# A decoder layer whose issue order is computed: other assumed costs for matmuls, small products and scans

## The chip, the cores and the metric

The kernel runs on one core of one Trainium2 chip. The time is device microseconds (us) of one execution. A core has a tensor engine (PE, with the loading of weights shown apart as PEld), a vector engine (DVE), a scalar engine (ACT), GpSimd (POOL) and SyncE (SP), which here starts the transfers (DMA). Each engine works through its own list of instructions in order; between engines, an instruction waits until what it reads has been written and what it overwrites has been read.

## The reference

One layer on 512 tokens of width 1024: a half-step gated feed-forward part (FFN 1), a mixer, cross-attention into 256 memory tokens, and a second half-step feed-forward part (FFN 2), each with a norm before and after. The mixer is where the change acts. It has eight heads of forgetting attention and four of a gated delta rule:

```python
def causal_conv_silu(x, w):                    # four taps over the tokens, then silu
    ...
cq, ck, cv = jnp.split(qkv, ...)               # after the convolution
q = l2_norm(cq...);  k = l2_norm(ck...)
beta = jax.nn.sigmoid(gb)
g = -jnp.exp(gdn_a_log) * jax.nn.softplus(ga + gdn_dt_bias)
...
L = jnp.where(strict, jnp.einsum('bhncd,bhnsd->bhncs', k_beta, k) * decay, 0.0)
A = L + jnp.eye(CHUNK)
u = lax.linalg.triangular_solve(A, v_beta, left_side=True, lower=True)
w = lax.linalg.triangular_solve(A, k_beta * jnp.exp(g)[..., None], left_side=True, lower=True)
...                                            # then a scan over the chunks of tokens
```

## The kernel before, in words

Large products are made in float32 by three float32r passes: a weight block of 128 x 1024 (`raw`) is split into a high part (`wh`, by ACT) and a low part (`wl`, by DVE, or now and then by POOL, see `nblock`), activations likewise, and PE multiplies high by high, low by high and high by low. Products run over 512 columns in the feed-forward parts, over 256 or 512 in the mixer.

The mixer, in the program's order:

- Gates (lines 771 to 870). A small product gives the logits; they are put in `zr`, turned by four PE transposes, worked on by DVE, ACT and POOL in `gw` (128 x 64), put in `yd`, turned back, and summed along the tokens by scans (`gc`, 128 columns a piece; `Fc`, 512 columns).
- Keys of four heads. The convolution adds three taps by DVE and one by POOL in `cy`; ACT takes a tanh into `cth`; DVE forms `co`. The same three tiles serve queries and values (`qv`, line 1005). `cR`, `cV`, `qe` and other small columns come from `smalls`, of which some are a power that POOL takes (`mhalf` is the exponent -1/2).
- The inverse of `A` (from line 990). The 32-row diagonal blocks of all heads go through memory, a block to a partition (`Lb`), and are solved by 31 steps on DVE: `Wb` is a product, `Tb` the update. The result returns by a DMA to `T` and is transposed by DVE to `X`. Products of 32 and of 64 rows on PE then double the blocks. `vb` are the values times beta, by ACT.
- The scans over chunks, the heads of forgetting attention, the output product, the mixer's last norm (`h`, `xn`), whose rows PE transposes (`xt`). The keys of the memory (`km`, from `mT`) are computed beside the last norm.

No engine's order is written out. Every instruction goes through the class `Issue`, which keeps what it reads and writes (`add`, line 119) and gives it an assumed cost in ns by its engine, its kind and its size (lines 159 to 177). `place` (line 190) puts instructions on the engines by these costs, of those ready the most urgent first; `settle` (line 226) does this ten times, backwards and forwards by turns, takes the result with the shortest assumed span, and ties each engine's instructions to that order. `AFTER` holds the assumed time from an instruction's end to the start of one that waits for it; `TICK` and `COLUMNS` model the PE clock. Some instructions are issued through `TK`, `VK`, `AK` and `QK`, which keep the order in which they are written. Because all instructions are called from one helper, every row of the profile has line 270 before, and 273 after; tiles tell them apart.

Of the kernel before, what the change touches and what calls it, by code (L numbers as in the profile page):

```python
# [17 lines left out]
S = 512  # L18
# [20 lines left out]
class Issue:  # L39
    """The order in which the engines issue.  # L40

    Every instruction is kept with what it reads and writes. At the end they are placed on the
    engines by a rough cost, backwards and forwards by turns, of those ready the most urgent
    first, and each engine gets its instructions in that order (as dependencies that need no
    semaphore).
    """

    # from the end of an instruction to the start of one that waits for it: on the same engine,
    # on the tensor engine, on another
# [7 lines left out]
    # the tensor engine's clock is halved after a tick with too few columns  # L57
    TICK, COLUMNS = 3413.3, 3072

    def __init__(self, tc):  # L60
        self.tc = tc
        self.ins = []
        self.unit = []  # the engine or queue that is held
        self.kind = []  # what the next one waits for
        self.cost = []
        self.columns = []
        self.pred = []
        self.writer = {}
        self.readers = {}
        self.bank = {}  # L70
        self.rings = {}
        self.first = {}
        self.touched = {}
        self.before = {}
        self.ring_of = {}
        self.grain = {}
        self.kept, self.after = {}, {}

    def engine(self, engine, unit, ordered=False):
        """ordered: what is issued through it keeps its order"""  # L80
        return _Issuer(engine, unit, self, ordered)

    def tile(self, pool, shape, dt, tag, bufs=1, name=None, grain=(32, 32)):
        """a tile, told apart by pieces of so many rows and columns"""
# [10 lines left out]
    def cells(self, x):  # L95
        """name, pieces touched, rows, free size"""
# [22 lines left out]
    def add(self, ins, unit, op, fp32):  # L119
# [4 lines left out]
        for group, cells_of, size_of in ((ins.ins, reads, sizes[0]), (ins.outs, writes, sizes[1])):  # L124
            for x in group:
# [5 lines left out]
                if name.startswith("psum"):  # L131
                    # one after another on a bank
# [31 lines left out]
        elif unit == "PE":  # L164
            passes = 4 if fp32 and op == "matmul" else 2 if fp32 else 1
            cost = max(size * passes * 0.41667, cols * 0.8333) + 2.6
# [3 lines left out]
        elif unit == "DVE":  # L170
            single = op != "transpose" and len(sizes[0]) - scalars == 1 and not psum
            cost = 68 + size * (6.3 if op == "reciprocal" else 0.521 if single else 1.042) + 61 * scalars
# [11 lines left out]
    def keep(self, unit):  # L184
        """the last instruction stays behind the last kept one of its engine"""
# [4 lines left out]
    def place(self, edges, waits, urgency, clock=False):  # L190
        """start of each instruction, on each unit the most urgent ready one first"""
# [68 lines left out]
class _Issuer:  # L260
    """an engine whose instructions are kept"""
# [19 lines left out]
def tile_decoder_layer(  # L281
# [38 lines left out]
    # slots of [128, 512], handed out by hand  # L320
# [20 lines left out]
    def move(src, dst, n=None):  # L341
        """free slots from one ring to another"""
# [14 lines left out]
    def bank(*ids):  # L357
        """the next PSUM bank of a ring of banks"""
# [20 lines left out]
    # that of some instructions stays as written  # L379
# [33 lines left out]
    def rstd_of(s0, s1):  # L413
        """(s0 + s1 + eps) ^ -1/2"""
# [16 lines left out]
    def wblock(ap):  # L431
        """now and then Pool takes the low part"""
# [10 lines left out]
    # the first loads, in the order in which they are needed  # L443
# [28 lines left out]
    def prenorm(src, g, dst):  # L472
        """rms_norm of a block of 128 rows, transposed and split into dst(half, part)."""
# [17 lines left out]
    def proj_t(wb, xT, ps, sl, first=True, by=1, mm=mm):  # L491
        """transposed product: ps[:, sl] += w_block^T x^T (float32 by three float32r passes, each
        over so many k at a time)."""
# [20 lines left out]
    def nat_product(ks, lhs, wdram, nh, evac, ntail, ts=tuple(range(NT)), last=None):  # L514
        """natural product: out[t, n*512:] = sum_k lhs(k)[:, t]^T w[k]; evac(n, t, ps).
        The last ntail blocks of k (two k each) finish the row blocks one after another."""
# [35 lines left out]
    def residual_epilogue(gidx, weight, nxt, final=False):  # L552
        """evac callback: h += weight * rms_norm(product) * gain; then nxt(t)."""
# [82 lines left out]
    # ================= FFN 1 =================  # L636
    xT = new_xT()

    def lead_in(ps, xT):
        """the first products, of rows not normed yet; returns the rows' factors, in all partitions"""  # L640
# [78 lines left out]
    # ================= mixer =================  # L719
# [30 lines left out]
    # wmt order: gates, gk of all heads, (gq, gv) per head, (fq, fk) per pair  # L750
# [20 lines left out]
    # gates: each of four groups of 32 rows holds a decay logit, two forget logits and a beta  # L771
    # logit, four rows each, and the same again for the low part of the weights; the logarithms are worked out by token, [128 tok, chunk, group, kind]
# [57 lines left out]
    def aug(src):  # L830
        """rows (-hi, -lo, 1, 1) and (1, 1, hi, lo) of a logarithm, whose product is its difference"""
# [15 lines left out]
    # per-token columns [128 tok, chunk, head]  # L847
# [49 lines left out]
    # the 32-row diagonal blocks of each head go through DRAM, a block to a partition and back  # L897
    NB = 32 * S + 32  # from a diagonal block to the next one of its 128 tokens
# [22 lines left out]
    def decay(pg, hh, which, dst):  # L921
        """exp of the decay between two tokens of a chunk: [query, key], or its transpose"""
# [23 lines left out]
    # keys of all heads: convolved, silu-ed, transposed [channel, token]; L of each head  # L946
# [43 lines left out]
    # T = (I + L)^-1, X = T^T: the diagonal blocks of all heads by substitution, with a block  # L990
    # to a partition; then blocks are doubled twice by products
# [13 lines left out]
    def qv(hh):  # L1005
        """queries and values; attention inside a chunk (transposed)"""
# [31 lines left out]
    def inverse(hh):  # L1038
# [17 lines left out]
        # blocks of 32 rows doubled, those of rows 0-63 and of rows 64-127  # L1056
# [515 lines left out]
```

## Time and profile before

| | before |
|---|---|
| timed runs | 1224.33, 1222.79, 1224.20 us, median 1224.2 us |
| profiled execution, span of the instructions | 1222.4 us |
| PE busy | 1192.9 us (98%) |
| PE loading weights | 1002.6 us (82%) |
| DVE busy | 642.7 us (53%) |
| ACT busy | 493.0 us (40%) |
| POOL busy | 128.6 us (11%) |
| DMA | 120.32 MB, 98 GB/s |
| chain that ended last | PE 87%, DVE 7%, DMA 2%, issue 2%, ACT 2% |
| mean granted PE clock | 0.995 of full speed |

The shares are averages over the whole span, in which stages with different limits lie. The profiled execution is one of many; its span runs from the first to the last instruction, and the timed runs hold what lies around it too.

In a timeline, a row is the start in us, the time of one group in us, the engine, the line, the operation, the tile written and the tiles read with their shapes, and how many instructions the row holds; in brackets the idle time before it and what ended that. A matmul's time holds its pass through the array, and the next begins before it ends; its cost in a stream of matmuls is the interval between starts.

### The profile page before, as it was taken

What the parts mean: (1) busy time and instruction counts of PE and PEld (TensorE: products, weight loads), DVE (VectorE), ACT (ScalarE), POOL (GpSimd) and SP (SyncE); (2) the same over time, 40 slices, a digit from 0 to 9 for tenths busy, and PEclk for the clock granted to TensorE, in tenths of its full rate; (3) what the DMA queues carried; (4) which work ended last, traced back from release to release, by engine and by line L of the source; (5) the groups of instructions that cost most, each with busy time, mean ns of one, the idle gap of its engine ahead of it and who ended that gap; (6) DMA issues with size and microseconds to landing.
All of it is one profiled execution on the core that took longest, in us unless ns stands there. A gap on an engine that the chain in (4) does not pass through costs nothing.

```text
span 1222.4 us, 15630 instructions
## 1 busy us (share of the span) xinstructions
PE 1192.9 (98%) x6078; PEld 1002.6 (82%) x6078; DVE 642.7 (53%) x1152; ACT 493.0 (40%) x1024; POOL 128.6 (11%) x121
## 2 busy tenths in 40 slices
PE   7999999999999899899999999999999999999997
PEld 7888888888888687788787888888988888888886
DVE  5655455442327979469975744546634334342323
ACT  5323223222226564368974644435422323222221
POOL 1000000000001432222020442012000000000000
PEclk9999999999999999999999999999999999999999
DMA  5332322333333231211214253222432332333321
GB/s 192 122 100 90 103 88 102 103 103 104 109 101 104 87 113 57 91 54 54 73 60 164 91 181 118 79 67 65 125 103 88 102 97 93 104 107 100 102 71 69
DMA packets 41753, 120.32 MB, mean 98 GB/s; under 512 B 9424, under 2 KB 9680, under 8 KB 41680
## 3 DMA queue, kind: packets, MB, share of 16 engines
q1 hardware_dynamic: 41168, 119.20, 30.9%
q8 instruction: 47, 0.77, 0.3%
q0 software_dynamic: 512, 0.13, 0.1%
q14 instruction: 26, 0.21, 0.1%
HBM read 114.73 MB, written 4.46 MB: 98 GB/s over the span
## 4 chain that ended last, share of the span: by engine, by line
PE 87%; DVE 7%; DMA 2%; issue 2%; ACT 2%; SPq 0%; POOL 0%; DVEq 0%; POOLq 0%; ACTq 0%
PE psum L270 87%; DVE Wb L270 1%; DVE Tb L270 1%; DMA mr<-in_mem_dram 1%; DVE wl L270 1%; DVE gw L270 1%; DMA raw<-in_wkvk_dram 1%; DVE co L270 1%; DVE xn L270 1%; DVE cy L270 0%; SPq L270 0%; DMA h<-in_x_dram 0%; DVE smalls L270 0%; DVE pt L270 0%; DVE h L270 0%
## 5 line engine op out<-in xcount | busy, mean ns | idle before, releaser
L270 PE MATMUL psum<-xt,wh 128*128 128x512 f32 (+1 forms) x2064 | 599.4, 374 | 0.3 <-ACT wh L270 0.2
L270 PEld LDWEIGHTS psum<-xt,wh 128*128 128x128 f32 x2064 | 373.6, 190 | 63.5 <-ACT wh L270 0.5
L270 ACT ACTIVATE wh<-raw 128x1024 fp32r<-128x1024 f32 (+1 forms) x202 | 213.0, 1056 | 526.0 <-PE psum L270 293.3
L270 PE MATMUL psum<-xt,wl 128*128 128x512 f32 (+1 forms) x1016 | 376.6, 375 | 0.8 <-DVE wl L270 0.7
L270 DVE TENSOR_TENSOR wl<-raw,wh 128x1024 fp32r<-128x1024 f32 (+1 forms) x176 | 216.3, 1230 | 275.8 <-ACT wh L270 275.2
L270 PEld LDWEIGHTS psum<-xt,wl 128*128 128x128 f32 x1016 | 190.9, 190 | 32.7 <-DVE wl L270 1.2
L270 PE MATMUL psum<-wh,hh 128*128 128x512 f32 x352 | 137.1, 390 | 0.0
L270 PE MATMUL psum<-wl,hh 128*128 128x512 f32 x352 | 137.1, 390 | 0.0
L270 PE MATMUL psum<-wh,hl 128*128 128x512 f32 x352 | 137.0, 389 | 0.0
L270 POOL TENSOR_TENSOR smalls<-smalls,mhalf 128x1 f32<-128x1 f32 (+1 forms) x38 | 26.5, 700 | 789.8 <-ACT smalls L270 784.0
L270 PEld LDWEIGHTS psum<-wh,hh 128*128 128x128 f32 x352 | 66.1, 188 | 13.8
L270 PEld LDWEIGHTS psum<-wh,hl 128*128 128x128 f32 x352 | 66.1, 188 | 13.6
L270 PEld LDWEIGHTS psum<-wl,hh 128*128 128x128 f32 x352 | 66.1, 188 | 13.6
L270 POOL TENSOR_TENSOR wl<-raw,wh 128x1024 fp32r<-128x1024 f32 x26 | 63.7, 2450 | 120.8 <-ACT wh L270 110.2
L270 PE MATMUL psum<-wh,xt 128*128 128x512 f32 x128 | 43.5, 409 | 0.4 <-DVE q L270 0.4
L270 DVE SCALAR_TENSOR_TENSOR hv<-s,psum 128x512 f32<-128x512 f32 x22 | 15.1, 688 | 53.7 <-PE psum L270 53.5
L270 DVE TENSOR_TENSOR tu<-psum,rb 128x512 f32<-128x512 f32 x22 | 15.2, 692 | 53.4 <-PE psum L270 53.3
L270 DVE TENSOR_TENSOR fg<-psum,gbc 128x512 f32<-128x512 f32 x32 | 22.0, 688 | 37.1 <-ACT u L270 37.1
L270 DVE TENSOR_TENSOR tg<-psum,rb 128x512 f32<-128x512 f32 x22 | 15.2, 692 | 44.5 <-PE psum L270 44.5
L270 ACT ACTIVATE u<-psum 128x512 f32<-128x512 f32 x32 | 19.0, 593 | 41.4 <-PE psum L270 41.4
L270 ACT ACTIVATE hh<-hv 128x512 fp32r<-128x512 f32 x44 | 27.4, 623 | 16.2 <-DVE hv L270 16.2
L270 DVE TENSOR_TENSOR hl<-hv,hh 128x512 fp32r<-128x512 f32 x44 | 30.1, 685 | 1.5 <-ACT hh L270 1.5
(232 smaller groups left out, 1431.3 us busy)
## 6 DMA issues: line engine op xcount, KB each, us to landing
raw<-in_f2gu_dram SPq DMA_DIRECT2D x44, 512.0 KB
raw<-in_f1gu_dram SPq DMA_DIRECT2D x43, 512.0 KB
raw<-in_f1d_dram SPq DMA_DIRECT2D x22, 512.0 KB
raw<-in_f2d_dram SPq DMA_DIRECT2D x22, 512.0 KB
raw<-in_wmt_dram SPq DMA_DIRECT2D x21, 512.0 KB
gbc<-in_gains_dram SPq DMA_DIRECT2D x16, 256.0 KB
raw<-in_wmn_dram SPq DMA_DIRECT2D x8, 512.0 KB
raw<-in_wout_dram SPq DMA_DIRECT2D x8, 512.0 KB
```

What stands on the lines that cost most here:

```text
L270: r = call(*args, **kw)
```

## The change

Three of the assumed costs are different; nothing else of what the program does is. For a float32r matmul (one pass) PE's constant is 13.3 ns in place of 2.6. A float32 matmul (four passes) with inputs of at most 32 rows counts half. A scan of DVE counts 2.04 ns per element in place of 1.042. The diff's other lines remove comments and docstrings.

```diff
         elif unit == "PE":
             passes = 4 if fp32 and op == "matmul" else 2 if fp32 else 1
-            cost = max(size * passes * 0.41667, cols * 0.8333) + 2.6
+            cost = max(size * passes * 0.41667, cols * 0.8333) + (13.3 if passes == 1 else 2.6)
+            if passes == 4 and rows <= 32:
+                cost /= 2
             columns = size * passes * rows / 128
...
         elif unit == "DVE":
             single = op != "transpose" and len(sizes[0]) - scalars == 1 and not psum
-            cost = 68 + size * (6.3 if op == "reciprocal" else 0.521 if single else 1.042) + 61 * scalars
+            each = {"reciprocal": 6.3, "tensor_tensor_scan": 2.04}.get(op, 0.521 if single else 1.042)
+            cost = 68 + size * each + 61 * scalars
```

The program has the same instructions before and after. Their order on PE, DVE, ACT, POOL and SP differs from about 350 to 880 us of the span; the feed-forward parts are practically as they were. Two places follow.

DVE at the gates, before: the end of the gate chain. `gw_430` are the gates, `yd_431` their copy for the transposes back, `co_460` a head's keys after the convolution, `cy_466` the taps of the next head, `smalls_63` small columns.

```order
L270 SCALAR_TENSOR_TENSOR gw_430_2964<-gw_430_2964 128x64 x7
L270 TENSOR_TENSOR gw_430_2964<-gw_430_2964 128x64
L270 TENSOR_TENSOR gw_430_2964<-gw_430_2964,coef_2750 128x64
L270 SCALAR_TENSOR_TENSOR co_460_3110<-cth_459_3104,cy_458_3102 128x512
L270 COPY yd_431_2988<-gw_430_2964 128x16x16
L270 TENSOR_SCALAR smalls_63<-smalls_63 128x4
L270 SCALAR_TENSOR_TENSOR cy_466_3154<-psum_64,cw_2744,cy_466_3154 128x511
```

The same place now:

```order
L273 SCALAR_TENSOR_TENSOR gw_430_2964<-gw_430_2964 128x64 x3
L273 SCALAR_TENSOR_TENSOR cy_466_3154<-psum_64,cw_2744,cy_466_3154 128x511
L273 SCALAR_TENSOR_TENSOR gw_430_2964<-gw_430_2964 128x64
L273 SCALAR_TENSOR_TENSOR cy_466_3154<-psum_64,cw_2744,cy_466_3154 128x510
L273 TENSOR_TENSOR gw_430_2964<-gw_430_2964 128x64
L273 TENSOR_TENSOR smalls_63<-smalls_63 128x4
L273 TENSOR_TENSOR cV_455_3078<-smalls_63,bN_2967 128x4
L273 TENSOR_TENSOR gw_430_2964<-gw_430_2964,coef_2750 128x64
L273 TENSOR_TENSOR smalls_63<-smalls_63,bN_2967 128x4
L273 COPY yd_431_2988<-gw_430_2964 128x16x16
```

The two `cy_466` steps and four small ones on `smalls` and `cV` stood behind `yd` and now stand ahead of it; `co_460` is further up. On PE, 17 more matmuls of 256 columns stand ahead of the transposes of `zr`, and between these and those of `yd` there are 37 matmuls of 256 columns and 29 of 512 in place of 54 and 17.

DVE at the first steps of the substitution, before. `Wb_449` and `Tb_3047` are its steps, `co_496` and `co_506` the queries of the first and the second head, `cy_504` the taps of the second, `wl_557` the low part of a weight block. Of the steps left out at the end, `co_506` stands behind the fifth `Wb` and `wl_557` behind the sixth `Tb`.

```order
L270 SCALAR_TENSOR_TENSOR co_496_3428<-cth_495_3422,cy_494_3420 128x512
L270 SCALAR_TENSOR_TENSOR cy_504_3492<-psum_64,cw_2744,cy_504_3492 128x511
L270 TENSOR_SCALAR qe_498_3439<-smalls_63 128x4
L270 SCALAR_TENSOR_TENSOR cy_504_3492<-psum_64,cw_2744,cy_504_3492 128x510
L270 TENSOR_TENSOR Wb_449_3048<-Lb_3046,Tb_3047 64x31
L270 TENSOR_TENSOR Tb_3047<-Tb_3047,Wb_449_3048 64x31
L270 TENSOR_TENSOR Wb_449_3048<-Lb_3046,Tb_3047 64x60
L270 TENSOR_TENSOR Tb_3047<-Tb_3047,Wb_449_3048 64x30x2
```

The same place now:

```order
L273 SCALAR_TENSOR_TENSOR co_496_3428<-cth_495_3422,cy_494_3420 128x512
L273 SCALAR_TENSOR_TENSOR cy_504_3492<-psum_64,cw_2744,cy_504_3492 128x511
L273 SCALAR_TENSOR_TENSOR cy_504_3492<-psum_64,cw_2744,cy_504_3492 128x510
L273 TENSOR_SCALAR qe_498_3439<-smalls_63 128x4
L273 SCALAR_TENSOR_TENSOR co_506_3500<-cth_505_3494,cy_504_3492 128x512
L273 TENSOR_TENSOR wl_557_3915<-raw_555_3912,wh_556_3914 128x1024
L273 TENSOR_TENSOR Wb_449_3048<-Lb_3046,Tb_3047 64x31
L273 TENSOR_TENSOR Tb_3047<-Tb_3047,Wb_449_3048 64x31
```

`co_506` and `wl_557` moved ahead of the first `Wb`. Other `co` among the later steps moved ahead too, by 4 to 11 places; the last `Tb` stands at the same place of DVE's list as before. At the mixer's last norm, POOL's last power stood behind two of its weight parts and now stands behind one, and the PE transposes of the last `xn` pair stand 46 matmuls of 256 columns earlier.

## Rows read from the trace of the kernel before

**Rows 1.** Waits of PE, whole run: what for, us in total, times, longest.

```profile
PE psum L270 <- DVE smalls L270: 4.6, 2, 4.0
PE psum L270 <- DVE X L270: 3.3, 1, 3.3
PE psum L270 <- ACT vb L270: 2.6, 1, 2.6
PE psum L270 <- DVE xn L270: 2.1, 2, 1.9
PE psum L270 <- DVE co L270: 1.3, 1, 1.3
...
PE psum L270 <- DVE wl L270: 0.7, 1, 0.7
```

**Rows 2.** Windows: length, busy PE PEld DVE ACT POOL, clock, DMA share, GB/s.

```profile
100.00:150.00 50.00, 50.00 (x222) 41.42 (x221) 26.30 (x34) 14.81 (x18) 0.00 (x0) 1.00 0.31 95
448.26:494.94 46.68, 44.05 (x210) 36.09 (x210) 44.84 (x88) 23.82 (x54) 14.41 (x9) 0.96 0.19 59
502.50:505.90 3.40, 3.40 (x15) 2.35 (x12) 0.71 (x1) 0.43 (x2) 0.10 (x1) 0.50 0.66 176
700.00:705.00 5.00, 5.00 (x44) 5.00 (x43) 2.89 (x5) 3.23 (x6) 2.90 (x2) 1.00 0.62 220
```

**Rows 3.** Timeline of DVE, the substitution and `X`: start, time, instruction.

```profile
448.26 0.19 DVE L270 TENSOR_TENSOR Wb<-Lb,Tb 64x31 f32<-64x31 f32 x1
...
448.72 0.97 DVE L270 TENSOR_TENSOR Wb<-Lb,Tb 64x60 f32<-64x60 f32 x1
...
452.86 1.21 DVE L270 TENSOR_TENSOR wl<-raw,wh 128x1024 fp32r<-128x1024 f32 x1
...
492.53 2.41 DVE L270 TENSOR_TENSOR Tb<-Tb,Wb 64x31 f32<-64x31 f32 x1
...
501.55 0.71 DVE L270 STREAM_TRANSPOSE X<-T 128x512 f32<-128x512 f32 x1 [5.48 <-DMA T<-dt]
```

**Rows 4.** Timeline of DVE at the gates.

```profile
397.68 0.21 DVE L270 TENSOR_TENSOR gw<-psum,gw 128x64 f32<-128x64 f32 x1
397.93 2.17 DVE L270 SCALAR_TENSOR_TENSOR gw<-gw 128x64 f32<-128x64 f32 x1
...
404.57 4.75 DVE L270 SCALAR_TENSOR_TENSOR gw<-gw 128x64 f32<-128x64 f32 x7
...
410.37 0.29 DVE L270 COPY yd<-gw 128x256 f32<-128x256 f32 x1
...
411.21 0.75 DVE L270 SCALAR_TENSOR_TENSOR cy<-psum,cw,cy 128x511 f32<-128x511 f32 x1 [0.47 <-ACT cth L270]
```

**Rows 5.** Timeline of POOL.

```profile
397.02 3.00 POOL L270 TENSOR_TENSOR wl<-raw,wh 128x1024 fp32r<-128x1024 f32 x1 [0.34 <-ACT wh L270]
...
432.01 1.03 POOL L270 TENSOR_TENSOR smalls<-smalls,mhalf 128x4 f32<-128x4 f32 x1
...
500.26 2.34 POOL L270 TENSOR_TENSOR wl<-raw,wh 128x1024 fp32r<-128x1024 f32 x1 [5.37 <-issue]
```

**Rows 6.** Timeline of PE: the transposes.

```profile
395.38 0.60 PE L270 MATMUL psum<-ident,zr 128*128 128x128 f32 x4
...
410.80 1.08 PE L270 MATMUL psum<-ident,yd 128*128 128x128 f32 x4 [4.05 <-DVE smalls L270]
...
706.21 0.66 PE L270 MATMUL psum<-ident,xn 128*128 128x128 f32 x4
```

**Rows 7.** Timeline of DVE beside POOL's power at 432.01.

```profile
432.51 0.17 DVE L270 SCALAR_TENSOR_TENSOR cR<-smalls,eg 128x4 f32<-128x4 f32 x1
```

**Rows 8.** Timeline of ACT, ahead of the substitution and at the last norm.

```profile
441.95 1.06 ACT L270 ACTIVATE wh<-raw 128x1024 fp32r<-128x1024 f32 x1 [3.23 <-PE psum L270]
...
449.65 0.63 ACT L270 ACTIVATE cth<-cy 128x512 f32<-128x512 f32 x1 [0.58 <-POOL cy L270]
...
701.12 0.29 ACT L270 ACTIVATE smalls<-smalls 128x1 f32<-128x1 f32 x1
```

## The prediction, made before the changed kernel ran

> **What bounds the kernel now.** I read the waits of TensorE (PE) first, because the page's first line gives PE 98% of the span: any gain must come out of its waits, any loss must add one. Few count [rows 1]: 4.0 us of the 4.6 for the vector engine's (DVE) `smalls` are in truth for `yd`, the decay gates, as the instruction that waits shows [rows 6]; 3.3 us are for `X`, the inverted blocks; 2.6 us for the scalar engine's (ACT) `vb`; 2.1 us for `xn`, the last norm of the mixer. Then the windows [rows 2]: in the undisturbed stretch 222 matmuls of 512 columns take 50 us, 0.226 us each; further on 44 of 256 columns touch 5 us, of which the first and the last stick out, 0.12 us each. After the wait for `X` the granted clock is 0.50 of full speed, that is 1.2 GHz, for 3.4 us, so this wait costs 1.7 us more. Nearly all this lies between 400 and 510 us, and DVE is the engine that is late there: from the first step of the substitution (`Wb`, 448.26) to the end of the last (`Tb`, 492.53 + 2.41 = 494.94) [rows 3] it works 44.84 of 46.68 us [rows 2]. `X` follows 6.6 us later, behind a DMA [rows 3]. Everything ahead of `X` is held by that chain. After it PE is full again, but for the `xn` wait near 707.
>
> The last view is of one engine beside another. Small DVE steps on the gates, 0.21 us when alone, last 2.17 us or, seven together, 4.75 [rows 4], while Pool (GpSimd) takes a low weight part for 3.00 us [rows 5], and a second beside the seven. The first step lost 1.95, the seven about 4.75 - 7 x 0.25 = 3.0: 4.9 us of the gate chain are collisions. They are in no assumed cost, before or after.
>
> **The change, part by part.** No instruction goes or comes; PE's total work is the same. So I sum moved waits.
>
> *The assumed costs.* 213.3 + 13.3 = 226.6 ns for a 512-column float32r matmul is what the windows show; 216 was assumed. Better figures do not by themselves make a better order: an order that is just in time by them has no room for the 4.9 us.
>
> *Gates.* The new order puts 17 matmuls of 256 columns (0.12 us each) more ahead of the transposes of `zr`, with which the gate chain begins: 2.0 us. The wait of 0.7 us for `wl` just before [rows 1] goes, since that part is made earlier. `zr` starts at 395.38 [rows 6] + 2.0 - 0.7 = 396.7. From there to `yd` PE has 54 small and 17 large matmuls before, 37 and 29 now, and eight transposes (0.9 us as at 410.80): 37 x 0.12 + 29 x 0.226 + 0.9 = 11.9 us, so it comes for `yd` at 408.6. DVE's chain took from 397.68 to 410.66 [rows 4], 13.0 us. DVE starts about 0.4 later (`zr` is 1.3 later, of which a weight part that DVE did in between now fills some 0.9 beforehand), and gets two `cy` steps of 0.75 and four small ones in front of `yd`: + 2.1. That is 413.2 with the same collisions, 415.4 if two more steps fall under Pool. PE waits 5 to 7 us, not 4.05 [rows 6].
>
> A row bears on the collisions. Beside Pool's power of four numbers (432.01, 1.03 us [rows 5]) a DVE step with two SBUF inputs, `cR`, took 0.17 us [rows 7]: no wait, and I count none for powers. The Trainium skill ("SBUF — State Buffer", "Who interferes with whom") says that a DVE instruction with two SBUF inputs contends with a GpSimd instruction that reads SBUF, and that the second to issue blocks fully. By that the power now ahead of the last gate steps would hold them 1.0 us more, and the time below would be 1.0 us higher; the row speaks against it for powers, the stretched rows for it in weight parts.
>
> *From `yd` to the substitution.* Now 12 large matmuls fewer stand behind `yd` (2.7 us), and the wait for `co` (1.3 [rows 1]) goes. Before, PE took 31.2 us from `yd` (410.80) until it was done with the weights that ACT waits to overwrite (441.95 [rows 8]); now 27.2. 413.4 to 415.6 + 27.2 puts that at 440.6 to 442.8: ACT is 1.4 us early to 0.8 late, I take 0.3 early.
>
> Here the order hurts. `co` of the second head's queries and a weight part `wl` now stand before the first `Wb`; they stood nine and twelve places behind. The `co` needs ACT's `cth`, over at 449.65 + 0.63 = 450.3 [rows 8]; a weight's high part `wh` follows on ACT at once (1.06 as at 441.95, to 451.3), then `wl` on DVE (1.21 to 1.3, as at 452.86 [rows 3]), to 452.65. DVE runs in order: the first `Wb` can't start at 448.26 but 4.4 us later. Behind it the chain has these two fewer, 0.7 + 1.2 = 1.9 us; the second `Wb`, which took 0.97 beside an add of Pool (448.72 [rows 3]), where by the first's 0.19 some 0.25 would do, finds Pool done: 0.7. Net 4.4 - 1.9 - 0.7 = 1.8 later, with ACT's 0.3 early 1.5.
>
> One more term stands at its end. Pool's part at 500.26 follows a weight block that waits for PE's last matmuls ahead of `X` [rows 5]. PE arrives there earlier, since `vb` (2.6 [rows 1]) is no longer waited for: the `co` that held it up is eleven places earlier. Pool's 2.34 us may then fall onto the last steps, as one did on the step at 492.53 [rows 3]. Nothing to 2.2 us; I take 0.8. `X` is 1.5 + 0.8 = 2.3 us later, bounds 1.8 - 1.4 = 0.4 and 1.8 + 0.8 + 2.2 = 4.8. The gain on `vb` and `co` is swallowed: PE just waits longer for `X`, some 9 us. What the clock does after so long a wait no row shows. The nearest is the 3.4 us at half after 3.3 us [rows 2], which is there already: the same again adds nothing, one more such stretch 1.7 us. I take 0.5, nearer to the row.
>
> *Heads of attention, 510 to 650.* The order is nearly the old one; PE's waits there are too short for [rows 1], but for 1.3 us in four. I take 0, bounds -1.5 and +1.5.
>
> *Last norm.* The transposes of the last `xn` pair move 46 matmuls of 256 columns up, 5.5 us: from 706.21 [rows 6] to 700.7. Pool's power for them moves ahead of a weight part, behind which it stood. ACT's part of the sum is done at 701.12 + 0.29 = 701.4 [rows 8]; the power (at most the 1.03 of [rows 5], about half for one number) and one `xn` step of 0.75, as `cy` in [rows 4], put it at 702.7 to 703.2. PE waits 2.0 to 2.5, against 2.1 before [rows 1]. The new pair again meets a Pool part within 0.1 us: with a collision, 1.95 as in [rows 4], +1.7 after what the old one lost; without, and with ACT's sum ahead of its weight part, -0.5. I take +0.4.
>
> Sum: 2.3 + 0.5 + 0 + 0.4 = 3.2 us. The profiled execution's span is 1222.4 us; the median of the timed runs, 1224.2, is 1.8 above it, taken as constant: 1222.4 + 3.2 + 1.8 = **1227.4 us**. Its own range is -0.1 (0.4 + 0 - 0.5, all early) - 1.5 = -1.6 to 4.8 + 1.7 + 1.5 + 1.7 = +9.7: 1222.6 to 1233.9.
>
> **The rivals.**
>
> *Faster: the collisions don't come again.* What delays the gates are two Pool parts that start within 1 us of a gate step. Two `cy` steps with an input in PSUM now stand between gate steps, and could lie under Pool instead. Without the 4.9 us `yd` is there at 408.3 to 410.5, PE hardly waits, and all that ACT hands on is up to 5 us earlier: `X` 1.8 - 5.0 = -3.2, the last norm -0.5, so 1224.2 - 3.7 = 1220.5. Against it: Pool's queue is unchanged here and its parts still follow the same ACT instructions.
>
> *No difference that can be told.* The early end of each bound: ACT 1.4 early, no Pool part at the end, no collision in the last norm: 0.4 + 0.5 - 0.5 = 0.4, 1224.6 us. For it: DVE's work ahead of `X` is the same set of instructions, so an idle stretch filled before it is won behind it.
>
> *Slower by more.* DVE now has the heads' `co` 4 to 11 places earlier among the `Wb` and `Tb` steps. If PE or ACT is 2 us late with one, the chain stands, twice in the stretch: 1227.4 + 4 = 1231.4. It decides from a lateness of ACT of over 1 us at 442. Against it: DVE's 44.84 of 46.68 us [rows 2] leave it little to wait for, and the order before had `co` steps in the same chain.
>
> **How the numbers follow.** About 0.2% (2.4 us) is what a measurement of this kernel can tell from no change: below 1221.8 is faster, above 1226.6 slower. Forecast case 0.40, of which 0.05 falls below 1226.6; slower by more 0.12; no difference 0.25; faster 0.23. That gives slower 0.47, same 0.30, faster 0.23. The forecast case's bounds and the upper rival set the high end, 1232.5; the low end goes into the faster rival until about a tenth is left out, 1219.5. Cases of both signs hold the chance; beside it stands the forecast's own range above.
>
> **What would show it.** In the profile after: PE's wait for `yd` over 4 us; the first `Wb` near 452 with DVE idle before the `co` that stands ahead of it; no wait of PE for `vb`; a wait for `X` of 8 to 10 us, ended near 504; a wait for the last `xn` pair. The forecast is wrong if the gate steps show no stretched rows, if the first `Wb` starts before 450, or if `X` comes before 502.

## The result and the profile after

The changed kernel took 1236.81, 1236.86 and 1237.83 us, against a median of 1224.26 us for the kernel before: a ratio of 1.0111 (95% interval 1.0094 to 1.0127). Another chip gave 1237.74 us (four executions) against 1223.90 (21), 1.0114 (1.0090 to 1.0137). It is slower, as forecast, but by 12.6 us here and 13.8 on the other chip (medians) instead of 3.2, and outside the range of 1219.5 to 1232.5. (One execution of the changed kernel took 4221.71 us, one of `cut_bab` below 4222.52, and both are left out: in the trace of the first, 63 matmuls fill the 50 us from 100 on, in which 222 run otherwise [rows 2], with no fall of the granted clock on record, and why is not known.) The profile below is of an execution of 1236.01 us, with a span of 1234.1.

PE's waits in it, as in [rows 1]: what for, us in total, times, longest.

```profile
PE psum L273 <- DVE yd L273: 5.0, 1, 5.0
PE psum L273 <- DVE xn L273: 3.7, 2, 2.7
...
PE psum L273 <- DVE X L273: 3.5, 1, 3.5
PE psum L273 <- ACT vb L273: 3.1, 2, 2.1
...
PE psum L273 <- DVE ml L273: 1.4, 2, 1.2
PE psum L273 <- DVE pt L273: 1.2, 2, 1.0
```

The waits for `yd` and `xn` are one to two us longer each, that for `X` is hardly longer, and that for `vb` has stayed. They don't make the 11.7 us by which the span is longer (1234.1 against 1222.4). What does is in the profile's slices. The line of the clock, a digit for each of 40 equal slices in tenths of full speed, after; before, every digit of it is a 9:

```profile
PEclk9999999999999999699999999999999999999999
```

The 6 is the slice from 494 to 525 us, where PE resumes behind `X`. The windows there (columns as in [rows 2]), first of the changed kernel:

```profile
501.20:525.10 23.90, 23.18 (x152) 17.03 (x152) 6.45 (x16) 6.40 (x22) 0.58 (x1) 0.50 0.24 81
```

and of the kernel before, behind the stretch of 3.4 us of [rows 2]:

```profile
505.90:525.00 19.10, 19.06 (x195) 16.04 (x195) 11.06 (x31) 10.88 (x40) 0.94 (x3) 1.00 0.28 95
```

In both PE is never idle for long. Before, the granted clock is back at full (2.4 GHz) after 3.4 us; after, it stays at half (1.2 GHz) for 23.9 us. 20.5 us more at half are 10.2 us lost, and PE's idle time, its span less its busy time, grows by 2.4 (1222.4 - 1192.9 = 29.5 before, 1234.1 - 1202.2 = 31.9 after): together a little over the 11.7.

What PE does in that stretch, changed kernel (timeline: start, time, instruction). The wide matmuls take 0.43 us each at half, and among them stand the small products that double the blocks of the inverse:

```profile
501.92 0.63 PE L273 MATMUL psum<-X,L 32*32 32x32 f32 x8 [3.48 <-DVE X L273]
502.48 0.80 PE L273 MATMUL psum<-wl,xt 128*128 128x512 f32 x1
503.07 1.05 PE L273 MATMUL psum<-wh,xt 128*128 128x512 f32 x2
...
506.87 0.63 PE L273 MATMUL psum<-X,L 32*32 32x32 f32 x8
507.44 1.22 PE L273 MATMUL psum<-wh,xt 128*128 128x512 f32 x2
508.45 0.63 PE L273 MATMUL psum<-wl,xt 128*128 128x512 f32 x1
509.01 0.63 PE L273 MATMUL psum<-Qs,T 32*32 32x32 f32 x8
```

On the gates, DVE of the changed kernel, to be laid beside [rows 4]:

```profile
404.90 2.87 DVE L273 SCALAR_TENSOR_TENSOR gw<-gw 128x64 f32<-128x64 f32 x3
...
408.54 0.74 DVE L273 SCALAR_TENSOR_TENSOR gw<-gw 128x64 f32<-128x64 f32 x3
...
411.07 1.05 DVE L273 TENSOR_TENSOR smalls<-smalls,bN 128x4 f32<-128x4 f32 x1
412.03 0.28 DVE L273 COPY yd<-gw 128x256 f32<-128x256 f32 x1
```

and POOL there:

```profile
404.77 2.40 POOL L273 TENSOR_TENSOR wl<-raw,wh 128x1024 fp32r<-128x1024 f32 x1
408.66 1.02 POOL L273 TENSOR_TENSOR smalls<-smalls,mhalf 128x4 f32<-128x4 f32 x1 [1.50 <-DVE smalls L273]
410.90 1.19 POOL L273 TENSOR_TENSOR cy<-cy,cth 128x509 f32<-128x509 f32 x1 [1.22 <-DVE gw L273]
```

The collisions came again: three steps lost 2.1 us under a weight part, `smalls` 0.9 under an add of 509 columns. Further up two more steps were held up, in rows not shown: a `co` took 2.51 us at 397.39 (0.68 alone) and a gate step 1.08 at 403.78 (0.19 before). That is 5.7 us in all, against 4.9 before. Beside the power at 408.66 no step of DVE was held up.

At the substitution (DVE of the changed kernel, against [rows 3]):

```profile
448.19 0.69 DVE L273 SCALAR_TENSOR_TENSOR co<-cth,cy 128x512 f32<-128x512 f32 x1 [1.87 <-ACT cth L273]
449.13 1.22 DVE L273 TENSOR_TENSOR wl<-raw,wh 128x1024 fp32r<-128x1024 f32 x1 [0.26 <-ACT wh L273]
450.28 0.20 DVE L273 TENSOR_TENSOR Wb<-Lb,Tb 64x31 f32<-64x31 f32 x1
...
494.18 0.18 DVE L273 TENSOR_TENSOR Tb<-Tb,Wb 64x31 f32<-64x31 f32 x1
...
501.15 0.71 DVE L273 STREAM_TRANSPOSE X<-T 128x512 f32<-128x512 f32 x1 [5.66 <-DMA T<-dt]
```

`co` and `wl` do hold up the first `Wb`, by 2.0 us (448.26 before). But the chain from there to the end of the last `Tb` is 2.6 us shorter (44.08 against 46.68), so `X` comes 0.4 us earlier than before, not 2.3 later.

### The profile page after: what moved, and what is told of

Read it like the earlier page. It is cut to its first block, busy times and chain, and to the rows that moved or that the text cites. A ratio compares the mean times of both kernels' runs of the same rounds, so it can differ in the third digit from the quotient of the medians.

```text
span 4219.8 us, 15643 instructions
## 1 busy us (share of the span) xinstructions
PE 4209.4 (100%) x6078; PEld 2435.7 (58%) x6078; DVE 630.4 (15%) x1152; ACT 506.7 (12%) x1024; POOL 124.9 (3%) x121
## 4 chain that ended last, share of the span: by engine, by line
PE 99%; issue 0%; DMA 0%; SPq 0%; ACT 0%; DVE 0%; DVEq 0%; POOLq 0%; POOL 0%
PE psum L273 99%; DMA h<-in_x_dram 0%; SPq L273 0%; DVE h L273 0%; ACT u L273 0%; DVEq L1571 0%; POOLq L1571 0%; POOL smalls L273 0%; ACT smalls L273 0%
## 5 line engine op out<-in xcount | busy, mean ns | idle before, releaser
L273 PE MATMUL psum<-xt,wh 128*128 128x512 f32 (+1 forms) x2064 | 1833.7, 1026 | 0.0
L273 PEld LDWEIGHTS psum<-xt,wh 128*128 128x128 f32 x2064 | 898.2, 454 | 618.3 <-issue 612.5
L273 PE MATMUL psum<-xt,wl 128*128 128x512 f32 (+1 forms) x1016 | 1041.8, 1033 | 0.0
L273 PEld LDWEIGHTS psum<-xt,wl 128*128 128x128 f32 x1016 | 458.0, 456 | 311.7 <-issue 308.9
L273 PE MATMUL psum<-wh,hl 128*128 128x512 f32 x352 | 387.3, 1101 | 0.0
L273 PE MATMUL psum<-wl,hh 128*128 128x512 f32 x352 | 387.1, 1100 | 0.0
L273 PE MATMUL psum<-wh,hh 128*128 128x512 f32 x352 | 385.2, 1094 | 0.0
L273 PEld LDWEIGHTS psum<-wh,hl 128*128 128x128 f32 x352 | 151.4, 430 | 138.7 <-issue 138.7
L273 PEld LDWEIGHTS psum<-wh,hh 128*128 128x128 f32 x352 | 151.4, 430 | 136.2 <-issue 135.9
L273 PEld LDWEIGHTS psum<-wl,hh 128*128 128x128 f32 x352 | 149.5, 425 | 138.2 <-issue 138.2
```

Of the source, the lines that this page charges most:

```text
L273: r = call(*args, **kw)
```

## The experiments

Each time stands beside that of the kernel before on the same chip. With several, the mean granted clock of single executions is given. It helps to tell outcomes apart, but it counts every stretch at half, also those in which PE would have waited anyway; where a stretch lies is known for the one execution of each kernel that has a trace.

**One cost at a time, and the changed kernel again.** The changed kernel itself was profiled a second time, and each of its three edits was made alone.

> The changed kernel unchanged, for a profile that can be read. Known so far: it is 13 us slower, and its mean granted clock is 0.986 against 0.995, that is about 34 us at half clock against 12, 22 us more, which costs some 11 us. Theory A (clock): PE's waits in total grow by at most 3 us, and the rows show 20 us or more of additional time at granted clock 0.50, in one stretch longer than 3.4 us or in six or more stretches of 3.4 us; they begin behind a wait of PE for X or yd. Theory B (my forecast's mechanism, only larger): PE's waits for yd and X grow by 8 us or more in total, the first Wb starts near 452, and the time at half clock grows by less than 7 us.

Measured: clock 0.984 to 0.987 in four executions, and the one long stretch shown above; waits + 2.4 us. Theory A fits, in the form of one stretch; B falls: `Wb` at 450.3, waits far below 8 us.

```diff
# pe_only: only the constant of PE (against the changed kernel; half_only and scan_only take the other lines back)
-            if passes == 4 and rows <= 32:
-                cost /= 2
...
-            each = {"reciprocal": 6.3, "tensor_tensor_scan": 2.04}.get(op, 0.521 if single else 1.042)
+            each = {"reciprocal": 6.3}.get(op, 0.521 if single else 1.042)
```

> Only the constant of the one-pass matmuls (13.3 ns), the two other costs as before. Theory A1 (this constant moves nearly every product against the other engines, so it carries the change): 1233 to 1240 us, mean clock below 0.990. Rival A2 (each set of costs falls on some other order, and what it costs is decided by whether PE waits at yd, vb or X just then, not by which cost was corrected): anywhere from 1218 to 1240 us, with a time that follows the mean granted clock: 1222.4 us of span at 0.995, some 1.2 us more for each 0.001 less.

> Only the halved cost of four-pass products with inputs of at most 32 rows. It acts on few instructions, the products of the diagonal blocks behind X. Theory A1: within 2.4 us of before, 1222 to 1227 us, clock 0.994 to 0.996. Rival A2: its order on PE differs from before in some 480 listed lines, two thirds as many as the whole change's 700, so its time may lie anywhere from 1218 to 1240 us, following its clock.

> Only the cost of the scans (five instructions of DVE at the gates). Theory A1: within 2.4 us of before, 1222 to 1227 us. Rival A2: 587 listed lines of PE's order differ; anywhere from 1218 to 1240 us, following its clock. If it is as slow as the whole change, 1235 us or more, the gates' end (yd, gc, Fc) carries the loss.

Measured, against 1223.90 for before: the constant alone 1236.44 (ratio 1.0081, 1.0048 to 1.0114), halving alone 1233.97 (1.0064, 1.0037 to 1.0091), scans alone 1222.36 (0.9989, 0.9977 to 1.0001). A1 falls: the halving, which touches a few products, loses 10.1 us, nearly as much as the constant, which touches all (12.5). The constant alone has one execution of six at 1229.41 us with a clock of 0.995, the others lie at 1234.4 to 1237.6 with 0.986 to 0.988. And halving alone has two outcomes from one and the same program: two executions at 1223.28 and 1224.35 us with a mean clock of 0.995, eight at 1231.4 to 1237.3 with 0.983 to 0.988. Its profile has the stretch:

```profile
501.60:525.50 23.90, 23.77 (x148) 17.08 (x149) 6.56 (x17) 7.29 (x23) 0.37 (x1) 0.50 0.21 77
```

With the scans alone PE does not wait for `X` at all, and the same part of the program runs at full clock:

```profile
500.00:525.00 25.00, 25.00 (x223) 19.94 (x222) 13.79 (x35) 12.96 (x42) 3.52 (x4) 1.00 0.36 112
```

So the question became: is it the wait for `X`, and what brings the clock back?

**The wait filled.** In the changed kernel 14 matmuls of 512 columns are issued where PE stands still; the lines of the edit that tie them to that place in PE's order are left out here:

```diff
+                if hh == 0 and i == 0 and c == 0:
+                    for _ in range(14):
+                        r = nc.tensor.matmul(
+                            qp, xk(xT, 0, slice(0, P), 0)[:, 0], xk(xT, 0, full, 0), start=True, stop=True
+                        )
+                        issue.fill.setdefault(len(issue.ins), []).append(r.ins)
                 mm(qp[up, 32 * c : 32 * c + 32], ck(L, c)[dn, up], ck(X, c)[dn, dn], start=True, stop=True)
```

> The changed kernel's order with 14 matmuls of 512 columns more on PE, placed right ahead of the first product of X, where PE waits 3.5 us; they write the PSUM bank that the product of X then overwrites, so nothing that is computed changes. 14 x 0.2265 = 3.2 us, less than the wait. Theory C (the loss is PE's granted clock behind X, and it falls because PE stands still there): no stretch at 0.50 between 495 and 526, PE reaches the heads of attention some 12 us earlier than in the changed kernel, 1225 to 1228 us. Rival D (the products of 32 rows behind X hold the clock down by themselves, whatever came before): the clock still falls within 10 us of X and stays at 0.50 until about 525, 1235 to 1240 us.

Measured: 1230.09 us against 1224.01 (ratio 1.0055, 1.0037 to 1.0074; four executions, 1229.46 to 1232.76; clock 0.991 to 0.993). The order of PE's work is that of the changed kernel, `X` comes no earlier (its first product starts at 502.19, 501.92 unfilled), and in the 23 us behind it the clock doesn't fall:

```profile
502.00:525.00 23.00, 23.00 (x216) 18.55 (x216) 12.75 (x35) 12.04 (x43) 1.07 (x3) 1.00 0.37 111
```

Unfilled, the same 23 us of the changed kernel:

```profile
502.00:525.00 23.00, 23.00 (x151) 16.85 (x152) 5.79 (x15) 6.30 (x22) 0.00 (x0) 0.50 0.22 77
```

D falls: one and the same order runs wholly at either clock, and with the wait filled the clock stays up. Each against the kernel before on its chip, the changed kernel loses 13.8 us and the filled one 6.1: 7.7 us are this. The price named by C, 1225 to 1228, was missed: some 6 us have another cause. Where the time goes is seen from PE's first transpose of `gx`, at the end of the heads of attention (before, changed, filled: first and last start):

```profile
L270 PE MATMUL psum<-ident,gx x16: 271/273/330, 638.4 to 645.9; 128*128 128x128 f32 x16
L273 PE MATMUL psum<-ident,gx x16: 270/273/328, 648.2 to 655.6; 128*128 128x128 f32 x16
L277 PE MATMUL psum<-ident,gx x16: 270/273/329, 638.7 to 646.4; 128*128 128x128 f32 x16
```

From the first product of `X` (502.3, 501.9 and 502.2) that is 136.1, 146.3 and 136.5 us: the whole 10.2 us are lost there, and the fill brings 9.8 of them back. From `gx` to the last transposes of `xn` the filled kernel's trace loses 2.7 us to the changed kernel's (230.2 against 227.5): its clock is at half from 698.2 to 705.0 there, and that of the changed kernel's is not.

**What PE runs behind the wait.** Four changes of order and one of work; the order ahead of `X` stays, and the wait is not filled.

```diff
# after_dense6 (PE): the next six wide matmuls ahead of the second small group
+        pe = pe[:first] + [pe[n] for n in up] + [pe[n] for n in keep] + pe[up[-1] + 1 :]
...
# after_local and before_local: 48 places of PE, from one ahead of X's first product, in the other kernel's order
+        pe[k - 1 : k + 47] = sorted(pe[k - 1 : k + 47], key=rank.get)
...
# after_solve: all engines, 25 us of assumed time from X on
+        order = order[:x] + sorted(order[x:end], key=rank.get) + order[end:]
```

> The changed kernel's order, but on PE the next six matmuls of 512 columns stand ahead of the second group of small products behind X: twelve wide matmuls in a row there instead of six. PE's work is the same. Theory C, with the addition that the clock comes back if PE streams wide matmuls behind the wait, and stays down as long as small products are strewn among them: the stretch at 0.50 behind X is 3.4 or 6.9 us long instead of 23.9; 1226 to 1231 us. Rival D: the stretch stays over 17 us, 1234 us or more.

Measured: 1235.78 us against 1224.01 (ratio 1.0099, 1.0077 to 1.0121). The clock did come back, at 508.1, and fell again 3.4 us later for 10.2. The wide matmuls taken forward are missing there: of the 75 instructions that PE runs in these 3.4 us two are wide, and PE is idle for 0.51 us. Three windows of it:

```profile
501.20:508.10 6.90, 6.33 (x37) 4.64 (x39) 1.66 (x3) 0.65 (x2) 0.53 (x1) 0.51 0.76 269
508.10:511.50 3.40, 2.89 (x75) 2.22 (x70) 1.81 (x5) 2.78 (x10) 0.00 (x0) 1.00 0.04 14
511.50:521.70 10.20, 10.20 (x55) 8.33 (x53) 2.56 (x8) 2.51 (x9) 0.00 (x0) 0.50 0.00 0
```

> The changed kernel's order, but the 47 instructions of PE behind X in the order in which the kernel before has them: three matmuls of 512 columns change places, so that seven wide ones stand ahead of the second small group (six in the changed kernel, seven before). Everything else as in the changed kernel. If the order of these few decides: the stretch is 3.4 or 6.9 us, 1226 to 1231 us. If it is decided by when X comes against the end of the last stretch, or by what other engines do: over 17 us, 1234 us or more.

> The other way round: the kernel before, but the 47 instructions of PE behind X in the changed kernel's order (X one wide matmul later, six instead of seven wide ones ahead of the second small group, one between the third and the fourth). If the order of these few decides: the stretch at 0.50 behind X grows from 3.4 us to over 17, 1230 to 1236 us. If not: 1222 to 1226 us, as before.

> The changed kernel's order, but with what all engines do in the 25 us behind the first product of X (by assumed times) in the order of the kernel before. If the order in this stretch decides: a stretch at 0.50 of 3.4 or 6.9 us, 1227 to 1232 us (the other waits of the changed kernel remain, as with the filled wait: 1230). If not: 1235 us or more.

Measured: `after_local` 1238.11 us against 1224.01 (ratio 1.0103, 1.0068 to 1.0138; three of four executions at 0.985 to 0.986, one at 1230.26 with 0.991). `before_local` 1225.60 (ratio 1.0019, 1.0001 to 1.0036): six executions at 1222.5 to 1225.9, four at 1228.7 to 1230.7 with 0.985 to 0.990. `after_solve` 1235.37 against 1224.04 (1.0089, 1.0059 to 1.0119): three at 1234.9 to 1237.2, one at 1228.99 with 0.994. So the order of these few instructions does not settle it, and my expectation that it decides is not borne out. That it shifts how often the slow outcome comes is likely for `before_local` (four of ten, against seven of the 75 executions of the kernel before that are counted below); one good execution of four, against none of seven of the changed kernel, is too little to tell.

Two traces here say more than the times. PE's order ahead of `X` is that of the changed kernel in both (in `after_local` but for one wide matmul), yet its wait for `X` was 1.7 us in `after_local` and 1.9 in `after_solve`, not 3.5. Behind the first the clock was at half for 20.5 us, behind the second not at all:

```profile
503.30:523.75 20.45, 20.45 (x144) 15.14 (x142) 5.79 (x15) 5.84 (x21) 0.81 (x1) 0.50 0.24 81
501.60:525.00 23.40, 23.36 (x226) 19.37 (x227) 13.92 (x39) 12.49 (x46) 4.22 (x6) 1.00 0.35 111
```

So the length of the wait is itself not fixed by the order, and by itself it does not tell what the clock does behind it.

```diff
# after_strewn: three more wide matmuls ahead of each of six small groups behind X (two of the six; the others alike)
...
+            if hh < 2 and c == 0:
+                for _ in range(3):
+                    r = nc.tensor.matmul(qp, xk(xT, 0, slice(0, P), 0)[:, 0], xk(xT, 0, full, 0), start=True, stop=True)
+                    issue.fill.setdefault(len(issue.ins), []).append(r.ins)
             mm(qp[up, 64 * c : 64 * c + 64], ck(L, c)[dn, up], ck(X, c)[dn, dn], start=True, stop=True)
```

> The changed kernel's order with 18 matmuls of 512 columns more on PE, three ahead of each of six groups of small products behind X (each writes the PSUM bank that the group then overwrites); the wait for X is left as it is. At full clock they cost 18 x 0.2265 = 4.1 us. If the clock stays down because small products leave PE too thin at 1.2 GHz to get it back (theory C): the stretch at 0.50 behind X shrinks from 23.9 to 6.9 us or less, 17 us less at half is 8.5 us won, net 1231 to 1235 us, faster than the changed kernel with more work in it. If the stretch does not depend on what PE streams: 4.1 to 8.2 us slower, 1242 to 1246 us.

Measured: 1233.23 us against 1224.04 (ratio 1.0084, 1.0064 to 1.0104), 4.5 us faster than the changed kernel's 1237.74 with 4.1 us more of matmuls in it (four executions, clock 0.991 to 0.994). The wait for `X` is 3.5 us as in the changed kernel. The clock is down for 6.8 us and then stays up past the end of the heads of attention:

```profile
500.00:506.83 6.83, 5.34 (x40) 3.95 (x41) 1.85 (x3) 0.65 (x2) 1.37 (x1) 0.50 0.80 226
506.83:525.00 18.17, 18.17 (x157) 13.95 (x154) 7.04 (x20) 8.60 (x29) 0.00 (x0) 1.00 0.07 27
```

Nothing but wide matmuls was added, and the clock was 0.991 or more in all four executions, against 0.987 or less in all seven without them. So this run shows that, in this order and once the clock has fallen, the share of wide matmuls among the small products bears on how long it stays down. It does not show that it alone decides.

**The order cut at X.** Both orders are worked out in one program and joined at the first product of `X`:

```diff
+        x = next(n for n, i in enumerate(head) if self.unit[i] == "PE" and self.reads(i) == {"X", "L"})
+        done = set(head[:x])
+        order = head[:x] + [i for i in tail if i not in done]
```

> All engines in the changed kernel's order up to the first product of X, and in the order of the kernel before from there on. If the order behind X decides (theory C): the stretch behind X is 3.4 or 6.9 us, mean clock 0.993 or more, 1224 to 1229 us, of which the later yd and the waits ahead of X are worth 1 to 3. If the way in which PE comes to X decides: 0.987 or less, 1233 us or more.

> The other way round: before's order up to the first product of X, the changed kernel's from there on. If the order behind X decides: clock 0.987 or less and a stretch over 17 us in most executions, 1232 to 1238 us. If the way to X decides: 0.993, 1223 to 1229 us, of which the changed kernel's longer waits for the last xn are 1.6 us and for others some 2.

> Before's order up to the first product of X, the changed kernel's from there to the first transpose of gx (about 645 us), and before's again behind it. The kernel with the changed order from X to the end took 1230.3 us at an almost undisturbed clock, 6 us more than before. If these 6 lie in the last norm (PE's wait for the last xn 3.3 us instead of 1.9, and 3.4 us more at half clock behind it, together 3 to 4 us): 1225 to 1228 us, with the rest in the heads of attention. If all lies in the heads: 1229 to 1231 us. If all lies in the last norm: 1223 to 1225 us.

Measured, against 1224.04 for before: the changed order up to `X` (`cut_ab`) 1226.56 (ratio 1.0010, 0.9992 to 1.0028), in two groups: 1220.6 to 1222.2 at a clock of 0.993 to 0.995 (four), 1226.2 to 1228.5 at 0.988 to 0.992 (six). The changed order from `X` on (`cut_ba`): 1230.33 (1.0070, 1.0040 to 1.0101), four executions at 1229.0 to 1230.7 with 0.992 to 0.993, one at 1238.33 with 0.986. With the last norm in before's order too (`cut_bab`): 1226.21 against 1224.48 (1.0013, 0.9997 to 1.0028), one execution of ten at 1233.40 with 0.985.

Up to `gx` the last two have the same order, on PE instruction for instruction, and PE waits 3.0 and 2.9 us for `X`. One trace, that of `cut_ba`, has 3.4 us at half behind it, the other 20.5:

```profile
501.50:504.91 3.41, 3.41 (x18) 2.31 (x20) 0.71 (x1) 0.65 (x2) 0.25 (x1) 0.50 0.63 187
504.00:524.48 20.48, 20.48 (x138) 14.60 (x137) 5.15 (x13) 5.75 (x20) 0.00 (x0) 0.50 0.23 82
```

So the changed order behind `X` costs 6 us where the clock behaves as before: some 4.5 in the last norm and some 2 in the heads of attention, near the expectation's first case. The 2 are not clear of zero by the times alone; the traces bear them out (from `X` to `gx` 138.0 us in `cut_ba`, 136.1 before, with 3.4 us at half in both). Ahead of `X` it costs nothing when the clock holds (the four at 1220.6 to 1222.2; the expectation of the next section counted five). Neither half of the order alone brings the long stretch each time: six of ten executions with the changed order ahead of `X` lose some 6 us, by their mean clock with about 12 us more at half, but none of these has a trace; with the changed order behind `X` one of five is slow; with both, all seven (0.984 to 0.987). Of 75 executions of the kernel before, seven took over 1227 us (0.986 to 0.991).

**The wait filled in the others.** Seven wide matmuls ahead of `X` in the kernel with the changed order up to `X`, 13 in the kernel before; the edit is that above.

> The changed kernel's order up to X and before's behind it, with 7 matmuls of 512 columns more on PE right ahead of the first product of X, where that kernel waits 1.7 us. Without them it took 1220.6 to 1222.2 us in five of ten executions (mean clock 0.993 to 0.995) and 1226.2 to 1228.5 in the others (0.988 to 0.992). If the wait for X is what makes the clock fall for long in these others: nearly all executions at 1220 to 1223 us, clock 0.993 or more, median 1221 to 1222, which is 2 us faster than before. If the clock falls for another reason: two groups of times as without them.

> The kernel before with 13 matmuls of 512 columns more on PE right ahead of the first product of X, where it waits 3.3 us. If the clock behind X costs what the rows show, 3.4 us at half: 1.7 us faster, 1222 to 1223 us in the median, and no execution over 1226 us. If the wait is not what makes it fall: no change, 1224 us, with single executions up to 1231.

Measured, against 1224.48 (27 executions, up to 1230.44): `cut_ab_fill` 1220.81 us, ratio 0.9965 (0.9946 to 0.9983); nine executions of ten at 1218.5 to 1222.0, one at 1226.18. `before_fill` 1221.87 us, ratio 0.9972 (0.9960 to 0.9983), all twelve at 1219.7 to 1222.7. The median is 2.6 us lower, of which the stretch of 3.4 us explains 1.7. None of the twelve is slow; with four of 27 over 1227 us unfilled that fits, but twelve are too few to show that they can't come. One of `cut_ab_fill` does lie in the slower group. PE of `before_fill` behind `X`:

```profile
503.60:525.00 21.40, 21.34 (x212) 17.85 (x213) 12.03 (x32) 11.42 (x41) 1.35 (x4) 1.00 0.39 120
```

Both beat the two kernels, with the reference's computation and some products of no use added to it.

## Why the forecast was wrong

**What bounds the kernel.** Right: every us lost is one in which PE waits or runs at half clock.

**Gates.** Right in mechanism: the collisions came again and `yd` was there at 412.3 (412.03 + 0.28; forecast 413.2); PE waited 5.0 us (5 to 7). Both were about 1 us earlier than forecast, since `zr` started at 395.3, not at 396.7. The row on the power held: the gate steps beside it (408.54, three in 0.74 us) were not stretched, so the 1.0 us that the Trainium skill ("SBUF — State Buffer", "Who interferes with whom") would add did not come there; the small step at 411.07, whose two inputs lie in SBUF, did wait beside POOL's add, as the Trainium skill says.

**From `yd` to the substitution.** Right in kind, wrong in size. DVE stood idle ahead of `co` and the first `Wb` was late, but by 2.0 us instead of 4.4: ACT's `cth` was ready at about 448.2, not at 450.3. I had left ACT's end where it was, though the order of POOL and ACT ahead of it changed as well. The shorter chain behind came as forecast, by 1.9 + 0.7 = 2.6 us; the 0.8 for one more collision at its end did not. `X` then came 0.4 us early, not 2.3 late, and its first product at 501.9: below the 502 that the prediction itself named as a sign of being wrong. The waits for `vb` didn't go (3.1 us), so the gain that I had swallowed at `X` was not there, and the wait for `X` was 3.5 us instead of 9.

**The clock: the step that failed.** "The nearest is the 3.4 us at half after 3.3 us [rows 2], which is there already: the same again adds nothing, one more such stretch 1.7 us. I take 0.5, nearer to the row." It was 7.7 us by the filled wait, 10.2 by the rows: behind a wait of 3.5 us, hardly longer than the 3.3, the clock was at half for 23.9 us. I took the one execution that I could see for a property of the wait. What stood in the trace of before and wasn't read: behind `X` come 20 us in which wide matmuls are few and small products many. That PE's clock can run at either level all through them, no row of that trace shows; the later runs do. The Trainium skill ("TensorE: Matmul & The Clock Gate", "Part 1: The HAM clock gate (the "warmup" mystery)") says that the clock is set by how busy PE has recently been. By the window of 501.20 to 525.10, PE was busy for 23.18 of 23.90 us, as the profile counts it, and stayed at 1.2 GHz; the row speaks against busy time alone.

**Last norm.** A second term too small: forecast 0.4 us with a bound of 1.7 if the new pair of `xn` meets a POOL part; it did. DVE, then POOL, then PE of the changed kernel:

```profile
711.41 3.55 DVE L273 SCALAR_TENSOR_TENSOR xn<-h,smalls,gbc 128x512 f32<-128x512 f32 x2 [0.44 <-POOL smalls L273]
```

```profile
709.97 1.41 POOL L273 TENSOR_TENSOR smalls<-smalls,mhalf 128x1 f32<-128x1 f32 x1 [0.37 <-PE psum L273]
711.41 2.34 POOL L273 TENSOR_TENSOR wl<-raw,wh 128x1024 fp32r<-128x1024 f32 x1
```

```profile
714.35 0.66 PE L273 MATMUL psum<-ident,xn 128*128 128x128 f32 x4 [2.72 <-DVE xn L273]
```

The power ahead of the pair took 1.41 us, where the same took 0.54 at 694.11: it started beside DVE's `wl` of 1.22 us at 709.75. So the power itself can take longer beside a step of DVE with two inputs in SBUF; the forecast counted at most 1.03 for it.

The stage cost some 4.5 us by the cut kernels, since the 2.1 that I counted as there before [rows 1] were a chance of that one execution: in `before_local` and `before_fill`, which have before's order here, PE's waits for `xn` are 0.5 and 0.6 us. And the clock can fall behind this wait too. In the trace of the changed kernel (2.7 us) it doesn't; in the kernel cut at `X` with the changed order behind (3.3 us) it does:

```profile
706.30:709.71 3.41, 3.41 (x16) 3.41 (x17) 2.25 (x4) 1.19 (x2) 0.00 (x0) 0.50 0.52 161
```

**Heads of attention.** Forecast 0 with a bound of 1.5; measured 1.7 by the times (1226.21 against 1224.48, with an interval that includes no difference) and 1.9 by the traces, of which the rows show PE's waits for `pt` (1.2 us, before 0.2) and `ml` (1.4, before 0.7).

**Sum.** Clock behind `X` 7.7, last norm 4.5, heads 2, ahead of `X` nothing: 14.2 for the 12.6 and 13.8 measured. The 7.7 is against a kernel that has lost the 3.4 us at half of the kernel before too, so up to 1.7 us of the sum are not the change's; it fits no better than to some 1.5 us. In the two traces, the span is longer by -0.4 us up to `X`, 10.2 from there to `gx`, 2.3 from there to the last transposes of `xn` (863.6 and 875.7) and -0.4 behind: the 11.7. That the forecast had the right side is luck in the main: of its 3.2 us, the 2.3 at `X` did not come, and what came stood in it with 0.5 and 0.4. The rival "slower by more" had the right side and the wrong place.

**Still open.** What decides, in one execution, whether the clock is back after 3.4 us or after 20. The same program gives both. The order ahead of `X` and what PE runs behind it shift how often, but no run here isolates what in them does it, nor why one order ahead of `X` leaves PE a wait of 1.7 us in one execution and 3.5 in another.

## What to carry to other kernels

A wait of PE is priced by the work behind it too: where small products stand among few wide matmuls, a wait of 1.7 to 3.5 us cost anything from nothing to 10 us of clock here, and filling it with matmuls of no use was cheaper than waiting. An order computed from better figures is another order, not a better one, as long as what decides is outside the model (collisions of DVE with POOL) or hangs on times that it only assumes (the clock behind a wait): each of three corrections alone gave 1222, 1234 or 1236 us. One profile shows one execution; before a wait or a stretch in it carries a term, see whether other runs with the same order have it.

## What the runs showed of the hardware

The granted clock can hold either level over one and the same order of PE's work for over 20 us: 216 matmuls in 23 us at 1.00, 151 at 0.50, PE busy throughout in both (`after_fill` and the changed kernel). Behind nearly the same wait, in the same order, it was at half for 3.4 us in one execution (`cut_ba`) and for 20.5 in another (`cut_bab`). More work can make the kernel faster: 18 wide matmuls more, 4.5 us less; 13 more ahead of `X`, 2.6 us less than the kernel before.
